# The seven products of the up projection in another order, on one core

## The chip, the cores and the metric

The kernel runs on one core of a Trainium2 chip. What is measured is the device time of one execution in microseconds (us). The kernel before takes 2845.7 us (median of three runs, 2845.06 to 2845.85).

## The reference

One layer of a hybrid decoder on 512 prompt tokens and 8 sample tokens, all in float32: attention and a gated branch side by side, an output projection, then a feed-forward part. Only the first step of the feed-forward part is touched:

```python
h = rmsnorm(x, lw['ffn_norm_w']) @ lw['w_up']        # 2048 -> 2 x 5632
...
hc = cw[0] * hp[:, 0:L] + cw[1] * hp[:, 1:L + 1] + cw[2] * hp[:, 2:L + 2] + lw['conv_b']
hg, hu = jnp.split(hc, 2, axis=-1)
x = x + (jax.nn.silu(hg) * hu) @ lw['w_down']
```

## The kernel before

All weights come from memory as blocks of 8 tiles of 128x128 (512 KB). For each block that TensorE multiplies with, ACT makes a rounded copy `hi` (`cast_block`, L246) and DVE the remainder `lo` (`rest_block`, L252); a product uses both. `hi` and `lo` have three buffers each, so ACT may begin the copy of block w+2 when TensorE leaves block w-1.

The up projection runs over 44 pairs of output tiles. Each pair (a **turn** below) is done with a scheme of seven products in place of eight (`winograd` for the weights, `wpair` for the matmuls, L353). A product is one block: 8 tiles, three matmuls each, 24 matmuls of 128x260. The turn reads four raw blocks: r11, r21, r22, r12. Tile `L` starts as r11, tile `S` as r21, both with two buffers; r12 and r22 come into plain tiles `st` (three buffers). Products P1 and P7 use `L`, P5, P6 and P3 use `S`, P2 uses r12 and P4 uses r22. In between the tiles are changed in place:

- first sum: `S` += r22, an accumulating DMA of POOL (L274), before P5
- second sum: `S` += `L`, an addition on DVE (L276, "vsum"), between P5 and P6
- `L` += r21, an accumulating DMA of POOL, between P1 and P7
- third sum: `S` += r12, an accumulating DMA of POOL, between P6 and P3

The order is written by hand. `acts[w]` lists what happens at the start of block w; with v the number of the turn's first block, the entries stand at v-8 to v+1. `block_start` (L258) issues them: loads on SP (L264), then what was left for this block, then the copy of block w+2 on ACT and its remainder on DVE, and behind these the sums of the block (L274, L276), POOL's small preparations `hb` (L1257, L1258) and SP's store `fd` of a finished turn (L1298). Every engine and both DMA queues take their instructions in this order. A load on SP waits until the last user of its buffer is through.

The products of a turn share four accumulators; after a product ACT or DVE takes the running value (`snap` L364, L368, L372, L376, L377). P1, P6 and P7 share bank a, so P6 cannot start before P1's value is copied out. Beside the products DVE and ACT work off the convolution of the turn before (L1263 to L1286). `w_out`, the stage ahead, builds the operands X of the seven products in the order of `PRODUCTS` (L405, L406, L414 to L425).

Of the kernel before, what the change touches and what calls it, by code (L numbers as in the profile page):

```python
# [17 lines left out]
S = 512  # L18
# [28 lines left out]
GV_TILES = tuple(range(20, 28))  # L47
MIX_TILES = (Q_TILES[0],) + sum(((Q_TILES[i + 1], GV_TILES[i]) for i in range(7)), ()) + GV_TILES[7:] + GU_TILES
FF_CHUNKS = (11, 11, 11, 11)
PRODUCTS = ("P5", "P1", "P2", "P6", "P4", "P7", "P3")  # L50
BANK = {"P5": "b", "P1": "a", "P2": "c", "P6": "a", "P4": "d", "P7": "a", "P3": "b"}
KQ = KD // 2

# [25 lines left out]
class Stream:  # L79
# [28 lines left out]
    def winograd(self, name, n1, n2, ks):  # L108
        assert not self.open and len(ks) == 2 * BLK
        v = len(self.keys)  # L110
        r11, r21, r22, r12 = (self.block([(name, k, n) for k in kk])
                              for kk, n in ((ks[0::2], n1), (ks[0::2], n2), (ks[1::2], n2), (ks[1::2], n1)))
        for p in PRODUCTS:
            self.vblock([(name, p, n1, i) for i in range(len(ks) // 2)],
                        {"P1": ("L", r11), "P7": ("L", r11), "P2": ("st", r12), "P4": ("st", r22)}.get(p, ("S", r21)))
        acts = self.acts
        acts[v - 8].append(("load", "S", r21, r21))
        acts[v - 7].append(("sum", "S", r21, r22))
        acts[v - 6].append(("load", "L", r11, r11))
        acts[v - 4].append(("load", "st", r12, r12))  # L120
        acts[v - 2] += [("load", "st", r22, r22), ("vsum", "S", r21, ("L", r11))]
        acts[v - 1].append(("sum", "L", r11, r21))
        acts[v + 1].append(("sum", "S", r21, r12))

    def done(self):
        assert not self.open
# [45 lines left out]
class Kernel:  # L172
# [180 lines left out]
    def wpair(self, name, n1, n2, X):  # L353
# [21 lines left out]
        def c12():  # L375
# [5 lines left out]
                 "P3": [("dve", c12)]}  # L381
        for p in PRODUCTS:
            z = BANK[p]
# [797 lines left out]
    def w_out(self):  # L1181
# [12 lines left out]
        X, build = self.woperands(xb)  # L1194
        X.update({p: [None] * KQ for p in PRODUCTS})
        todo = [(p, i) for p in PRODUCTS[:5] for i in range(KQ)] + [(p, i) for i in range(KQ) for p in PRODUCTS[5:]]
        early = [(p, i) for i in range((KD - OUT_GROUP) // 2) for p in ("P5", "P1")]
# [39 lines left out]
        self.finish_fine()  # L1237
        while todo[0][0] in PRODUCTS[:3]:
            build(*todo.pop(0))
# [304 lines left out]
```

## Time and profile before

| | before |
|---|---|
| median of three runs | 2845.7 us |
| the profiled execution's own time | 2843.6 us |
| its span | 2841.9 us |
| granted TensorE clock, mean | 0.994 |
| TensorE busy | 2771.4 us (98%) |
| DVE busy, ACT busy | 1564.8 us, 1090.1 us |
| up projection on TensorE | from 1157.15 to 2116.25 us |

Times within the profile are in us from the start of the span. In the rows of the timeline stand the start, the busy time, engine, line, operation, what is written and read, how many instructions were merged, and in brackets the idle time ahead and what ended it. In the chain of waits a row gives start, length and what the chain passed through.

### The profile page before, as it was taken

Reading aid. Unit: us, or ns where it says so; the run is one execution under the profiler, and the core shown is the slowest. Engines: PE = TensorE matmul, PEld = TensorE weight load, DVE = VectorE, ACT = ScalarE, POOL = GpSimd, SP = SyncE. Lnnn points to the kernel's source line nnn. Section 1 sums busy time; section 2 is a strip of 40 time slices with the busy share of each in tenths; the row PEclk is TensorE's granted clock in tenths of the full one; section 3 lists DMA queues with packets and bytes.
Section 4 is the critical chain, followed back from the end, with each engine's and each line's share of the span. In section 5 each row is a group of like instructions: output and inputs, shape, how many; then the busy total and the mean of one; then the engine's idle time right before and its main releaser. Section 6 shows DMA issues by size and latency. Waiting matters only on the chain.

```text
span 2841.9 us, 53344 instructions
## 1 busy us (share of the span) xinstructions
PE 2771.4 (98%) x22836; PEld 2753.5 (97%) x22836; DVE 1564.8 (55%) x2309; ACT 1090.1 (38%) x1775; POOL 237.1 (8%) x381
## 2 busy tenths in 40 slices
PE   9999999999999999799999999999999999999999
PEld 9999999999999999799999999999999999999999
DVE  5666555443333434777777777777773333333533
ACT  5465542222222333545444454444452222232321
POOL 0111000000000000021112112112210000000000
PEclk9999999999999999899999999999999999999999
DMA  5223233222232345477777777767765333323232
GB/s 179 90 88 115 83 97 92 87 88 88 94 94 93 112 139 169 120 188 189 175 180 193 185 179 190 188 168 188 185 184 194 120 115 120 112 91 96 86 112 94
DMA packets 118095, 381.01 MB, mean 134 GB/s; under 512 B 13457, under 2 KB 14609, under 8 KB 117857
## 3 DMA queue, kind: packets, MB, share of 16 engines
q1 hardware_dynamic: 97344, 303.49, 33.0%
q0 software_dynamic: 20512, 74.11, 13.4%
q8 instruction: 179, 2.93, 0.4%
q14 instruction: 60, 0.48, 0.1%
HBM read 352.42 MB, written 25.12 MB: 133 GB/s over the span
## 4 chain that ended last, share of the span: by engine, by line
PE 66%; DMA 15%; DVE 8%; POOL 4%; issue 4%; ACT 2%; DVEq 0%; SPq 0%; ACTq 0%; POOLq 0%
PE mm L330 21%; PE mm L334 20%; PE mm L332 20%; DMA S<-in_w 15%; DVE lo L252 4%; POOL hb L1258 3%; ACT hi L246 2%; DVE S L276 2%; POOL S L274 1%; PE wa L391 1%; DVE hb L1283 1%; PE wb L391 1%; PE po L927 1%; PE s L864 1%; PE pt L909 0%
## 5 line engine op out<-in xcount | busy, mean ns | idle before, releaser
L252 DVE TENSOR_TENSOR lo<-st,hi 128x1024 fp32r<-128x1024 f32 (+1 forms) x398 | 484.8, 1219 | 591.9 <-ACT hi L246 589.9
L246 ACT CAST hi<-st 128x1024 fp32r<-128x1024 f32 (+1 forms) x398 | 415.2, 1044 | 746.7 <-PE mm L332 438.2
L330 PE MATMUL mm<-xnh,hi 128*128 128x260 f32 x1920 | 393.8, 287 | 5.2 <-ACT hi L246 5.2
L391 PE MATMUL wa<-X,hi 128*128 128x260 f32 x2112 | 388.1, 285 | 7.2 <-ACT sn L364 7.1
L332 PE MATMUL mm<-xnl,hi 128*128 128x260 f32 x1920 | 386.3, 282 | 0.0
L334 PE MATMUL mm<-xnh,lo 128*128 128x260 f32 x1920 | 386.3, 283 | 0.0
L391 PEld LDWEIGHTS wa<-X,hi 128*128 128x128 f32 x2112 | 326.5, 190 | 7.9 <-ACT sn L364 7.5
L330 PEld LDWEIGHTS mm<-xnh,hi 128*128 128x128 f32 x1920 | 295.2, 189 | 5.3 <-ACT hi L246 5.2
L332 PEld LDWEIGHTS mm<-xnl,hi 128*128 128x128 f32 x1920 | 299.5, 190 | 0.0
L391 PE MATMUL wa<-X,lo 128*128 128x260 f32 x1056 | 298.6, 283 | 0.0
L334 PEld LDWEIGHTS mm<-xnh,lo 128*128 128x128 f32 x1920 | 293.5, 188 | 0.0
L330 PE MATMUL mm<-fh,hi 128*128 128x260 f32 x1408 | 284.2, 283 | 3.5 <-DVE x L1378 3.5
L334 PE MATMUL mm<-fh,lo 128*128 128x260 f32 x1408 | 284.3, 283 | 0.0
L391 PE MATMUL wb<-X,hi 128*128 128x260 f32 x1408 | 264.9, 289 | 19.6 <-DVE xr L1208 9.6
L332 PE MATMUL mm<-fl,hi 128*128 128x260 f32 x1408 | 283.6, 283 | 0.0
L391 PEld LDWEIGHTS wb<-X,hi 128*128 128x128 f32 x1408 | 220.1, 192 | 26.3 <-ACT hi L246 16.0
L252 DVE TENSOR_TENSOR lo<-S,hi 128x1024 fp32r<-128x1024 f32 x132 | 158.0, 1223 | 141.2 <-ACT hi L246 137.6
L391 PE MATMUL wb<-X,lo 128*128 128x260 f32 x704 | 204.5, 290 | 28.4 <-DVE lo L252 28.4
L330 PEld LDWEIGHTS mm<-fh,hi 128*128 128x128 f32 x1408 | 217.6, 189 | 3.7 <-DVE x L1378 3.7
L334 PEld LDWEIGHTS mm<-fh,lo 128*128 128x128 f32 x1408 | 218.3, 189 | 0.0
L332 PEld LDWEIGHTS mm<-fl,hi 128*128 128x128 f32 x1408 | 217.3, 189 | 0.0
L391 PEld LDWEIGHTS wa<-X,lo 128*128 128x128 f32 x1056 | 200.2, 190 | 0.2 <-DVE lo L252 0.2
(287 smaller groups left out, 4951.6 us busy)
## 6 DMA issues: line engine op xcount, KB each, us to landing
st<-in_w SPq DMA_DIRECT2D x395, 512.0 KB, 3.6
S<-in_w POOLq DMA_DIRECT2D x88, 512.0 KB, 10.3
S<-in_w SPq DMA_DIRECT2D x44, 512.0 KB, 3.6
L<-in_w SPq DMA_DIRECT2D x44, 512.0 KB, 3.9
L<-in_w POOLq DMA_DIRECT2D x44, 512.0 KB, 8.3
fd<-hb SPq DMA_DIRECT2D x44, 260.0 KB, 2.2
fr<-fd SPq DMA_DIRECT2D x44, 260.0 KB, 4.0
x<-in_x SPq DMA_DIRECT2D x16, 260.0 KB, 6.1
```

Of the source, the lines that this page charges most:

```text
L246: self.nc.scalar.copy(self.hi[v][:, c], self.st[WS.src[v]][:, c])
L252: self.nc.vector.tensor_sub(self.lo[v][:, c], self.st[WS.src[v]][:, c], self.hi[v][:, c].bitcast(F32))
L274: self.nc.gpsimd.dma_start(self.st[kind, r], self.a["w"][src], accum_op=ALU.add)
L276: self.nc.vector.tensor_add(self.st[kind, r], self.st[kind, r], self.st[src])
L330: mm(ps[:, h, 0:HW], lhsT=whi, rhs=xh[:, h, :], start=start, stop=False)
L332: mm(ps[:, h, 0:HW], lhsT=whi, rhs=xl[:, h, :], start=False, stop=False)
L334: mm(ps[:, h, 0:HW], lhsT=wlo, rhs=xh[:, h, :], start=False, stop=stop)
L391: nc.tensor.matmul(ps(z), lhsT=w, rhs=x, start=new and i == 0 and q == 0, stop=i == len(X[p]) - 1 and q == 2, skip_group_check=True)
L864: nc.tensor.matmul(out, lhsT=self.cols(q, c), rhs=keys(kk, c), start=n == 0, stop=n == 1)
L927: nc.tensor.matmul(po[:, kb * 128:kb * 128 + w], lhsT=vv[:, kb * 128:(kb + 1) * 128], rhs=pp[:, o:o + w], start=kb == 0 and n == 0, stop=k ...
L1258: nc.gpsimd.tensor_copy(sv(k)[:, :, 0:2], self.sc[:, n, :].rearrange("p (b r) -> p b r", b=NS))
L1283: nc.vector.tensor_mul(fv[:, :, 0:HP], tg[:, 0:S].rearrange("p (h w) -> p h w", h=2), tu[:, 0:S].rearrange("p (h w) -> p h w", h=2))
```

## The change

The seven products are multiplied in the order P1, P5, P6, P2, P4, P7, P3 in place of P5, P1, P2, P6, P4, P7, P3. The load of `S` and its first sum stand one block earlier in the list; the vsum stands one block later, at v-1, ahead of the sum of `L`, which stays at v-1; the third sum stands one block earlier, at v. `w_out` builds the operands in the new order.

```diff
-PRODUCTS = ("P5", "P1", "P2", "P6", "P4", "P7", "P3")
+PRODUCTS = ("P1", "P5", "P6", "P2", "P4", "P7", "P3")
...
-        acts[v - 8].append(("load", "S", r21, r21))
-        acts[v - 7].append(("sum", "S", r21, r22))
+        acts[v - 9].append(("load", "S", r21, r21))
+        acts[v - 8].append(("sum", "S", r21, r22))
         acts[v - 6].append(("load", "L", r11, r11))
         acts[v - 4].append(("load", "st", r12, r12))
-        acts[v - 2] += [("load", "st", r22, r22), ("vsum", "S", r21, ("L", r11))]
-        acts[v - 1].append(("sum", "L", r11, r21))
-        acts[v + 1].append(("sum", "S", r21, r12))
+        acts[v - 2].append(("load", "st", r22, r22))
+        acts[v - 1] += [("vsum", "S", r21, ("L", r11)), ("sum", "L", r11, r21)]
+        acts[v].append(("sum", "S", r21, r12))
```

On DVE, around the vsum of one turn. Before (lo317 is P5, lo318 P1, lo319 P2, lo320 P6; L1283 and L1286 are the last step of the turn before, after which `fd` is stored; L372, L376 and L377 take accumulators of the turn before):

```order
L252 TENSOR_TENSOR lo317_17622<-S261_17403,hi317_17621 128x1024
L276 TENSOR_TENSOR S261_17403<-S261_17403,L260_17479 128x1024
L1283 TENSOR_TENSOR hb_1083_17451<-c1_1077_17311,c2_1080_17411 128x2x256
L1286 TENSOR_TENSOR hb_1083_17451<-c1_1077_17311,c2_1080_17411 128x2x4
L372 SCALAR_TENSOR_TENSOR c2_1090_17659<-wa_1084_17478,sn_1085_17481 128x260
L252 TENSOR_TENSOR lo318_17655<-L260_17479,hi318_17654 128x1024
L376 TENSOR_TENSOR c1_1087_17559<-wb_1082_17442,un_1089_17587 128x260
L377 TENSOR_TENSOR c2_1090_17659<-wd_1088_17586,un_1089_17587 128x260
L252 TENSOR_TENSOR lo319_17692<-st263_17549,hi319_17691 128x1024
L1263 TENSOR_TENSOR hb_1091_17687<-c2_1090_17659,R2_888_12943 128x512
L1264 TENSOR_TENSOR hb_1091_17687<-c2_1090_17659,R2_888_12943 128x8
L252 TENSOR_TENSOR lo320_17732<-S261_17403,hi320_17731 128x1024
```

Now, in the same place of the same turn on DVE (lo317 is P1, lo318 P5, lo319 P6, lo320 P2):

```order
L252 TENSOR_TENSOR lo317_17624<-L260_17480,hi317_17623 128x1024
L1283 TENSOR_TENSOR hb_1083_17452<-c1_1079_17344,c2_1080_17410 128x2x256
L1286 TENSOR_TENSOR hb_1083_17452<-c1_1079_17344,c2_1080_17410 128x2x4
L372 SCALAR_TENSOR_TENSOR c2_1090_17658<-wa_1082_17443,sn_1085_17482 128x260
L252 TENSOR_TENSOR lo318_17654<-S261_17373,hi318_17653 128x1024
L276 TENSOR_TENSOR S261_17373<-S261_17373,L260_17480 128x1024
L376 TENSOR_TENSOR c1_1089_17592<-wb_1084_17479,un_1087_17551 128x260
L377 TENSOR_TENSOR c2_1090_17658<-wd_1088_17586,un_1087_17551 128x260
L252 TENSOR_TENSOR lo319_17693<-S261_17373,hi319_17692 128x1024
L1263 TENSOR_TENSOR hb_1091_17688<-c2_1090_17658,R2_888_12948 128x512
L1264 TENSOR_TENSOR hb_1091_17688<-c2_1090_17658,R2_888_12948 128x8
L252 TENSOR_TENSOR lo320_17733<-st263_17549,hi320_17732 128x1024
```

The vsum has moved behind L1283, L1286, L372 and P5's remainder; P6's remainder has moved ahead of L1263, L1264 and P2's remainder.

On POOL, the same turn (S261 and L260) with the first sum of the next turn (S265). Before:

```order
L274 DMA L260_17479<-in_w 128x1024
L1257 MEMSET hb_1091_17687 128x2
L1258 COPY hb_1091_17687<-sct_12949 128x8x2
L274 DMA S265_17651<-in_w 128x1024
L1257 MEMSET hb_1093_17699 128x2
L1258 COPY hb_1093_17699<-sct_12949 128x8x2
L274 DMA S261_17403<-in_w 128x1024
```

And now on POOL:

```order
L274 DMA L260_17480<-in_w 128x1024
L274 DMA S265_17621<-in_w 128x1024
L1257 MEMSET hb_1091_17688 128x2
L1258 COPY hb_1091_17688<-sct_12954 128x8x2
L274 DMA S261_17373<-in_w 128x1024
L1257 MEMSET hb_1093_17700 128x2
L1258 COPY hb_1093_17700<-sct_12954 128x8x2
```

One pair of preparations now stands behind the third sum (S261) and no longer ahead of it. On SP the order of loads and stores within the turns is what it was.

## The prediction

> **What bounds the kernel now.** I read the busy times first, then the waits of TensorE, then the chain of waits through the stage that the change touches.
>
> ```profile
> PE 2771.4 (98%) x22836; PEld 2753.5 (97%) x22836; DVE 1564.8 (55%) x2309; ACT 1090.1 (38%) x1775; POOL 237.1 (8%) x381
> ```
>
> ```profile
> PE wb L391 <- DVE lo L252: 28.4, 39, 0.8
> PE wb L391 <- DVE xr L1208: 9.6, 1, 9.6
> PE wb L391 <- ACT hi L246: 9.3, 20, 1.0
> PE wa L391 <- ACT sn L364: 7.1, 2, 6.9
> ```
>
> TensorE sets the time, and nearly all that it waits for lies in the up projection (L391): twice some us at the entry, and then 39 times, about once a turn, for weights of bank b. Bank b serves P5 and P3. The idle time understates the loss, since ends of matmuls are modelled, so I take the spacing of turns from the chain of waits:
>
> ```profile
> 1186.99 5.73 PE wb L391 x48
> 1207.09 5.73 PE wb L391 x48
> 1227.19 2.88 PE wb L391 x24
> ...
> 2113.35 2.90 PE wb L391 x22
> ```
>
> The first three rows begin with P3 of turns 0, 1 and 2: 1207.09 - 1186.99 = **20.10 us** a turn, with no wait, 2.87 us a product. The last row is P3 of turn 43 from its third matmul (22 are left), which in turn 2 stood two matmuls (0.24 us of the 2.88) behind the start, at 1227.43. So 41 turns took 885.92 us where 41 x 20.10 = 824.1 would do: **61.8 us lost**, 1.5 a turn.
>
> ```profile
> 1229.89:1400.00 170.11, 162.89 (x1321) 160.20 (x1320) 124.64 (x174) 83.48 (x142) 34.48 (x56) 0.99 0.73 184
> 1800.00:2000.00 200.00, 190.90 (x1550) 187.80 (x1549) 146.34 (x201) 97.91 (x167) 38.44 (x63) 0.99 0.73 184
> ```
>
> In these two stretches the granted clock was 0.99 (third number from the end); 1% of 370 us is 3.7. I leave 3 us of the loss to the clock and count **58.5 us** as waits. What sets the 1.5 us shows the chain between two copies of P3's weights:
>
> ```profile
> by line: DMA S<-in_w 45.6%; issue 11.7%; DVE lo L252 11.3%; POOL hb L1258 8.3%; DVE S L276 5.2%; ACT hi L246 4.8%; POOL S L274 3.5%; DVE hb L1283 2.6%; PE wb L391 1.2%; POOL hb L1257 0.8%; DMA fr<-fd 0.6%; DVE c L372 0.6%; DMA st<-in_w 0.5%
> ...
> 1634.38 1.06 ACT hi L246
> ...
> 1645.43 10.11 DMA S<-in_w
> 1655.62 1.06 ACT hi L246
> ```
>
> It is a loop: the third sum lands, ACT copies P3's weights, DVE works through its queue up to P6's remainder, POOL issues the next third sum, which lands 10.11 us later. One turn of the loop is 1655.62 - 1634.38 = 21.24 us, more than TensorE's 20.10. So the loop sets the pace, and its parts are what the change is to be judged by.
>
> **The change, part by part.** I put 0 at 1634.38 and lay the new order on the rows of this turn.
>
> ```profile
> 1636.28 0.65 ACT L1279 ACTIVATE c<-c 128x536 f32<-128x536 f32 x1
> 1637.09 1.05 ACT L246 CAST hi<-L 128x1024 fp32r<-128x1024 f32 x1
> 1642.82 1.05 ACT L246 CAST hi<-S 128x1024 fp32r<-128x1024 f32 x1
> ...
> 1635.47 2.36 DVE L252 TENSOR_TENSOR lo<-S,hi 128x1024 fp32r<-128x1024 f32 x2 [3.54 <-ACT hi L246]
> 1637.86 1.22 DVE L276 TENSOR_TENSOR S<-S,L 128x1024 f32<-128x1024 f32 x1
> 1639.01 0.69 DVE L1283 TENSOR_TENSOR hb<-c,c 128x512 f32<-128x512 f32 x1
> 1640.15 1.21 DVE L252 TENSOR_TENSOR lo<-L,hi 128x1024 fp32r<-128x1024 f32 x1
> 1641.28 0.42 DVE L376 TENSOR_TENSOR c<-wb,un 128x260 f32<-128x260 f32 x1
> 1641.96 1.21 DVE L252 TENSOR_TENSOR lo<-st,hi 128x1024 fp32r<-128x1024 f32 x1
> 1643.91 1.23 DVE L252 TENSOR_TENSOR lo<-S,hi 128x1024 fp32r<-128x1024 f32 x1
> ```
>
> ```profile
> 1639.97 0.33 SPq L1298 DMA_DIRECT2D fd<-hb  x1
> 1640.39 0.38 SPq L264 DMA_DIRECT2D L<-in_w  x1
> 1640.82 2.70 SPq L264 DMA_DIRECT2D st<-in_w  x2
> ...
> 1641.66 0.87 POOL L274 DMA_DIRECT2D L<-in_w  x1 [17.05 <-DVE lo L252]
> 1643.16 0.86 POOL L274 DMA_DIRECT2D S<-in_w  x1
> 1645.43 0.86 POOL L274 DMA_DIRECT2D S<-in_w  x1 [0.26 <-DVE lo L252]
> ```
>
> *DVE up to the sum of L.* Remainders of P3 and the first product end at +3.45, as now (P1's in place of P5's, which has the same size). L1283 follows at +3.48, the time at which the vsum starts today; it needs L1279, which ends at 1636.93 = +2.55. From L1283 to the start of the next remainder are 1640.15 - 1639.01 = 1.14 us, so P5's remainder runs from +4.62 to +5.83; its copy, in the place of today's copy at 1637.09, ends at +3.76. The vsum then starts at +5.76 (starts here follow 1.14 apart) and ends at +6.98. The sum of `L` comes 0.30 us after the DVE row that frees it (1641.66 against 1640.15 + 1.21): **+7.28**, to the hundredth what it is today (1641.66). The vsum's move costs nothing there: the pieces only change places.
>
> *The third sum.* P6's copy waits for the vsum: +7.04 to +8.09. L376 and L377 (0.68 us up to the next start) fit beside it. P6's remainder runs +8.13 to +9.36; today it starts at 1643.91 = +9.53 and ends at +10.76, because P2's remainder (1641.96) and two rows of the convolution stand ahead and its copy (1642.82) must wait until TensorE has left P5. POOL follows 0.29 us behind: **+9.65 against +11.05**, 1.40 us sooner. POOL is free by then: the sum of `L` at +7.28, the next turn's first sum 0.87 behind, and one pair of preparations, which today lets the following sum start 2.27 us after the one before it (1643.16 to 1645.43, DVE's wait included). With today's 10.11 us it lands at +19.8 and the loop closes in **19.9 us, below 20.10**.
>
> *The queue under it.* The 10.11 us are no property of the sum alone:
>
> ```profile
> 1640.50:1645.00 4.50, 4.50 (x40) 4.50 (x40) 4.44 (x7) 1.44 (x3) 3.34 (x6) 1.00 0.89 279
> 1645.00:1651.00 6.00, 6.00 (x53) 6.00 (x52) 3.85 (x7) 3.05 (x6) 1.03 (x2) 1.00 1.01 239
> 1651.00:1654.50 3.50, 3.50 (x32) 3.50 (x31) 2.69 (x3) 1.43 (x5) 0.00 (x0) 1.00 1.03 207
> 1654.50:1658.00 3.50, 2.74 (x24) 2.49 (x22) 1.30 (x2) 2.38 (x3) 0.00 (x0) 1.00 0.05 8
> ```
>
> The last two numbers of a row are the busy share of the DMA engines and GB/s. From SP's store at 1639.97 until the third sum is in, the 16 DMA engines are full (shares 0.89, 1.01, 1.03, and 0.05 behind it): three loads, the store and three sums share them. So a sum issued sooner lands sooner only if the full stretch also starts sooner. It does: the store needs L1283, which moves from 1639.01 (+4.63) to +3.48, and the two loads behind it on SP move with it, 1.15 us. If the stretch keeps its whole length, the loop takes 21.24 - 1.15 = **20.09**. The second of the two `st` loads waits for P2's remainder, which now comes behind P6's, some 2.5 us later; that takes bytes from before the sums and can only help them. The load of `S` keeps its place: it waits for P3's remainder (+2.3) either way, and SP's order is the same. "A block sooner" is thus worth nothing for the load, and the first sum, 0.6 us earlier, is not waited for.
>
> The Trainium skill speaks against the change here ("Trainium Kernel Development and Optimization", Key Constraints): DMAs of SP, ACT and POOL run on the same 16 DMA engines and interleave, so issuing from several engines saves only issue time. The trace agrees that they are shared (share 1.01 with loads and sums together). By that rule alone the third sum would land as long after the sum of `L` as today, and nothing would be won; that is the second rival below.
>
> *TensorE's side.* If P3 starts at +1.1 (copy done) and ends at +4.95 (its remainder comes at +2.3), P6, now third, is due two products later, at 4.95 + 2 x 2.87 = +10.7; its weights are ready at +9.36, 1.3 us to spare. P1's value in bank a is copied out right behind P6's copy (+8.09), in time for it. Next late would be P6, then nothing: P7's `L` lands with the first of the three sums. Once TensorE is the slower one, the sums are issued earlier against its position and the margin of P3 grows. So the steady turn should be 20.1 us: **-58.5 us**.
>
> *The entry.* This happens once.
>
> ```profile
> 1175.68 0.80 PE L391 MATMUL wa<-X,hi 128*128 128x260 f32 x2 [6.86 <-ACT sn L364]
> 1174.02 1.33 ACT L405 CAST X<-xb 128x260 fp32r<-128x260 f32 x4 [3.93 <-DVE xb L425]
> 1171.94 1.77 DVE L456 RECIPROCAL ry<-rv 128x260 f32<-128x260 f32 x1
> ```
>
> The wait of 9.6 us is for the last tile of the stage ahead and stays. In turn 0 P6 waits 6.86 us for P1's copy, which stands on ACT behind operands X that hang on a reciprocal of 1.77 us. Now P1's copy comes a block sooner, ahead of that; P6 comes a product (2.87) sooner as well, and P4's weights meet the reciprocal instead. Bounds: 6.9 us gained (wait gone) to 5 us lost (P6 meets the operands of P2, P4 and its own, at 0.4 us a step, one block earlier). I take the value near the reciprocal: **-2 us**.
>
> **The sum.** Profiled execution: 2843.6 - 58.5 - 2 = 2783. The median of the runs (2845.7) lies 2.1 above it, so the forecast for the runs is **2785 us**, 2774 to 2797 with the entry's bounds, a few us of clock and single stalls.
>
> **The rivals.**
> - *The loop shortens but stays above 20.10.* For it: 20.09 is no margin, and the full stretch varies (the clock aside, a turn lost 1.5 us on the mean, this one 1.14). Against it: the freed `st` load. At the middle between 20.1 and 21.24, half of the gain remains: 2845.7 - 29 - 2 = 2815.
> - *The change moves the issue and not the landing.* If the queue is served in order from the sum of `L` on, the third sum lands 1655.6 - 1641.66 = 13.9 us behind it. That issue stays at +7.28, so the loop stays 21.2: 2844, no change. Against it: SP's loads, which fill the first part of that stretch, do move.
> - *Slower: the vsum holds the sum of `L`.* It now stands directly ahead of it, behind P5's remainder, which can be copied only once TensorE has left P7. If that chain on DVE slips, the sum of `L` and the two behind it slip too. It decides from +7.28 plus what the stretch gains (1.15), +8.4; a slip of 1.15 + 1.22 (one more vsum's length) gives 41 x 1.22 = 50 us: 2896. Against it: the copy at +3.76 is 0.9 us ahead of DVE.
>
> **How the numbers follow.** Forecast 0.70, partial loop 0.15, landing unmoved 0.08, slower 0.07. The range takes the forecast whole with 2 us of the entry's lower end, and the partial case but its worst third: 2772 to 2828. A measurement of this kernel can tell about 0.2% (5.7 us) from no change: faster 0.85, same 0.08, slower 0.07.
>
> **What would show it.** Right: turns spaced 20.1 us, no waits of bank b for `lo` or `hi` in the steady state, ACT's copy of P3 no longer the last thing ahead of TensorE, the third sum issued 1.4 us sooner after P3's copy. Wrong: the sum of `L` issued later than +7.3 against P3's copy; a third sum that takes over 11 us; a new wait of bank a (P6) in every turn; P3 of turn 0 later than 1191, where it stood at 1186.99.

## The result, and the profile after

| | before | after |
|---|---|---|
| median of the runs | 2845.8 us (4 runs, 2845.1 to 2847.1) | 2798.5 us (4 runs, 2789.0 to 2799.9) |
| ratio of the times, 95% interval | | 0.9826 [0.9804, 0.9848] |
| profiled execution, its span | 2843.6 us, 2841.9 us | 2797.9 us, 2796.1 us |
| granted clock | 0.994 | 0.995 |

The kernel is 47 us faster, 13 less than the 60 that were forecast. It lies between the forecast (2785) and the first rival (2815: the loop shortens but stays above TensorE's pace).

From the page of the changed kernel its line of busy times, and then its waits of TensorE:

```profile
PE 2756.6 (99%) x22836; PEld 2747.3 (98%) x22836; DVE 1566.4 (56%) x2309; ACT 1091.2 (39%) x1775; POOL 218.4 (8%) x381
```

```profile
PE wb L391 <- DVE lo L252: 9.3, 16, 1.1
PE wa L391 <- DVE xr L1208: 9.0, 1, 9.0
...
PE wa L391 <- ACT sn L364: 3.6, 1, 3.6
...
PE wb L391 <- ACT hi L246: 1.7, 3, 0.8
```

Waits of bank b for `lo` have fallen from 39 times to 16, those for `lo` and `hi` together from 37.7 us to 11.0, but they have not gone. The starts of the turns tell it better than idle time. From the start of turn 1 to that of turn 43 the 42 turns took 59.9 us more than 42 x 20.10 before and take 20.7 us more now. Sixteen turns run at 20.13 or 20.14 us, without a wait; 26 take 20.2 to 23.5, and what they wait for is P3's weights. Turn 0 went from 32.5 to 29.5 us. These two make 42 of the 46 us between the profiled executions; the last turn gives 0.8, and most of the rest is that the up projection begins 2.3 us sooner (1154.88 against 1157.15); that start varies between 1154.9 and 1158.8 over all profiled kernels of this document, in both orders, and is not put down to the change.

One turn of the loop, in the timeline of the changed kernel, from P3's copy on ACT to the next (0 at 1587.05, as the prediction counted):

```profile
1587.05 1.05 ACT L246 CAST hi<-S 128x1024 fp32r<-128x1024 f32 x1 [4.38 <-DMA S<-in_w]
...
1589.76 1.05 ACT L246 CAST hi<-S 128x1024 fp32r<-128x1024 f32 x1
1594.15 1.05 ACT L246 CAST hi<-S 128x1024 fp32r<-128x1024 f32 x1 [3.33 <-DVE S L276]
...
1607.57 1.05 ACT L246 CAST hi<-S 128x1024 fp32r<-128x1024 f32 x1 [4.36 <-DMA S<-in_w]
```

```profile
1590.41 0.68 DVE L1283 TENSOR_TENSOR hb<-c,c 128x512 f32<-128x512 f32 x1
...
1591.56 1.22 DVE L252 TENSOR_TENSOR lo<-S,hi 128x1024 fp32r<-128x1024 f32 x1
1592.81 1.23 DVE L276 TENSOR_TENSOR S<-S,L 128x1024 f32<-128x1024 f32 x1
...
1595.23 1.23 DVE L252 TENSOR_TENSOR lo<-S,hi 128x1024 fp32r<-128x1024 f32 x1 [0.52 <-ACT hi L246]
```

```profile
1591.38 0.33 SPq L1298 DMA_DIRECT2D fd<-hb  x1
1591.80 0.38 SPq L264 DMA_DIRECT2D L<-in_w  x1
1592.23 6.39 SPq L264 DMA_DIRECT2D st<-in_w  x2
```

```profile
1594.57 0.86 POOL L274 DMA_DIRECT2D L<-in_w  x1 [17.42 <-issue]
1595.10 1.22 POOL L274 DMA_DIRECT2D S<-in_w  x1
...
1596.75 1.16 POOL L274 DMA_DIRECT2D S<-in_w  x1
```

The engines do what was worked out: L1283 at +3.36 (forecast +3.48), the vsum at +5.76 (+5.76), P6's remainder at +8.18 (+8.13), the third sum at +9.70 (+9.65). But P3's next copy comes at 1607.57 = +20.52 and not at +19.9: the third sum lands 10.7 us after its issue, where it was 10.1. The DMA engines are as full as before:

```profile
1592.00:1597.00 5.00, 5.00 (x44) 5.00 (x43) 4.45 (x7) 2.38 (x3) 2.43 (x5) 1.00 0.92 293
1597.00:1603.00 6.00, 6.00 (x52) 6.00 (x52) 5.31 (x9) 4.27 (x9) 1.32 (x4) 1.00 1.04 204
1603.00:1606.50 3.50, 3.50 (x31) 3.50 (x31) 2.36 (x4) 0.21 (x3) 0.00 (x0) 1.00 0.89 227
1606.50:1610.00 3.50, 3.39 (x29) 3.18 (x27) 1.35 (x2) 2.43 (x3) 0.00 (x0) 1.00 0.03 6
```

### The profile page after: what moved, and what is told of

It is laid out like the page before. It is cut to its first block, busy times and chain, and to the rows that moved or that the text cites. A ratio compares the mean times of both kernels' runs of the same rounds, so it can differ in the third digit from the quotient of the medians.

```text
span 2796.1 us, 53337 instructions
## 1 busy us (share of the span) xinstructions
PE 2756.6 (99%) x22836; PEld 2747.3 (98%) x22836; DVE 1566.4 (56%) x2309; ACT 1091.2 (39%) x1775; POOL 218.4 (8%) x381
## 3 DMA queue, kind: packets, MB, share of 16 engines
q0 software_dynamic: 20512, 74.11, 13.9%
## 4 chain that ended last, share of the span: by engine, by line
PE 75%; issue 16%; DMA 5%; POOL 2%; DVE 2%; ACT 1%; SPq 0%; POOLq 0%; ACTq 0%; DVEq 0%
PE mm L330 21%; PE mm L334 21%; PE mm L332 21%; DMA S<-in_w 4%; PE wa L391 4%; PE wb L391 3%; POOL S L274 1%; PE wc L391 1%; PE wd L391 1%; DVE lo L252 1%; POOL hb L1258 1%; PE po L927 1%; ACT hi L246 1%; PE s L864 1%; POOL L L274 1%
## 5 line engine op out<-in xcount | busy, mean ns | idle before, releaser
L391 PE MATMUL wa<-X,hi 128*128 128x260 f32 x2112 | 389.9, 285 | 12.7 <-DVE xr L1208 9.0
L246 ACT CAST hi<-S 128x1024 fp32r<-128x1024 f32 x132 | 138.5, 1049 | 304.3 <-DMA S<-in_w 153.0
```

Source lines behind the costliest of these rows:

```text
L246: self.nc.scalar.copy(self.hi[v][:, c], self.st[WS.src[v]][:, c])
L391: nc.tensor.matmul(ps(z), lhsT=w, rhs=x, start=new and i == 0 and q == 0, stop=i == len(X[p]) - 1 and q == 2, skip_group_check=True)
```

## The experiments

Each ran three rounds beside the kernel before, whose medians on those chips were 2843.6 to 2845.6 us. The theories in the expectations: **Q**, the full DMA engines decide when the third sum lands; **I**, it lands a fixed time after its own issue, which the new product order moved. The others are named where they stand.

**e1: the first sum behind the third.** Against the changed kernel:

```diff
-        acts[v - 8].append(("sum", "S", r21, r22))
+        acts[v - 7].append(("sum", "S", r21, r22))
```

> The changed kernel with the first sum back at v-7, where it now stands on POOL directly behind the third sum of the turn before it, no longer ahead of it. Theory Q (the DMA engines are full from the loads to the third sum, so what stands ahead of the third sum decides when it lands): 512 KB less ahead of it, about 2.5 us sooner, at some 12.5 to 13 us after the start of the turn in place of 13.5 to 17; no P3 waits, turns of 20.13 us, 2798 - 20 = 2778 us (2774 to 2786). Rival I (the landing follows the third sum's own issue by 10 to 11 us, and the new product order moved that issue): issue unchanged at +4.6, time unchanged, 2798 us.

Measured: **2778.7 us**, ratio to before 0.9768 [0.9754, 0.9783]. TensorE does not wait in the steady turns: it is busy throughout these windows, and the two sums of `S` now go out together, the third first:

```profile
1190.00:1390.00 200.00, 200.00 (x1672) 200.00 (x1671) 161.91 (x220) 109.63 (x181) 43.21 (x70) 1.00 0.78 196
...
1790.00:1990.00 200.00, 200.00 (x1671) 200.00 (x1670) 161.39 (x218) 107.37 (x179) 43.07 (x70) 1.00 0.79 198
```

```profile
1592.06 0.86 POOL L274 DMA_DIRECT2D L<-in_w  x1 [15.53 <-issue]
...
1594.25 1.76 POOL L274 DMA_DIRECT2D S<-in_w  x2 [0.26 <-DVE lo L252]
```

The time is Q's. The landing was sooner than expected, mostly 10 to 11 us after the start of the turn (median 10.0, latest 12.6) and not 12.5 to 13. So the "block sooner" of the first sum does harm: it puts 512 KB ahead of the sum that is waited for.

**e4: r22's load behind that of the next S**, so that it runs in the idle time behind the third sum. No sum is moved:

```diff
-        acts[v - 2].append(("load", "st", r22, r22))
-        acts[v - 1] += [("vsum", "S", r21, ("L", r11)), ("sum", "L", r11, r21)]
+        acts[v - 1] += [("load", "st", r22, r22), ("vsum", "S", r21, ("L", r11)), ("sum", "L", r11, r21)]
```

> The changed kernel with the load of r22 one place later on SP, behind the load of the next S, so that it runs while the DMA engines are idle and no longer beside the sums. No sum is moved. Theory Q: 1.5 us of work leaves the full stretch ahead of the third sum, which lands about 1 us sooner; most P3 waits go: 2778 to 2790 us. Rival I: the third sum's issue is unmoved, 2798 us.

Measured: **2781.4 us** [ratio 0.9759, 0.9792]. A plain load that nobody waits for, taken out of the stretch, is worth 17 us, and no sum goes out sooner for it (the third 6.4 us behind the store, 5.4 in the changed kernel): Q.

**e5: e1 and e4 together.**

> e1 and e4 together: first sum behind the third and r22's load behind that of the next S. In e1 TensorE already runs its turns at 20.13 us without a wait, so Theory Q expects nothing more: 2778 us (2775 to 2782). A rival that sees e1's and e4's gains as two separate ones would expect 2798 - 20 - 17 = 2761 us.

Measured: **2778.7 us** [ratio 0.9757, 0.9786], as e1 alone; the two cure the same wait.

**e2: the old order, the first sum a block sooner.** One part of the change alone, on the kernel before (load at v-9, first sum at v-8):

> The kernel before with one part of the change alone: load and first sum of S one block sooner. Theory Q and rival I agree: the third sum's issue (+11 us after the copy of P3) and the bytes ahead of it stay, so 2845 us (2840 to 2850). Rival F (the gain came from the first sum begun sooner): about 2800 us.

Measured: **2846.9 us**, ratio 1.0007 [0.9997, 1.0016]. This part of the change is worth nothing.

**e3: the old order, the first sum behind the third.**

```diff
-        acts[v - 7].append(("sum", "S", r21, r22))
+        acts[v - 6].append(("sum", "S", r21, r22))
```

> The kernel before, old product order, with the first sum one block later (v-6), so that it stands behind the third sum on POOL. Theory Q: the third sum lands about 2.5 us sooner, P3 no longer waits, but P5 follows directly and waits for the first sum that is now last; the loop closes over P5 at about 20.0 to 20.4 us: 2790 to 2805 us. Rival I (the product order is what counts, the issue of the third sum is unmoved): 2845 us, or slower by what P5 waits.

Measured: **2796.4 us** [ratio 0.9813, 0.9842], in the range of Q. One place in POOL's queue gives the old product order the same gain as the whole change. The waits that are left stand elsewhere than expected: about half of them at P1, the product behind P5, and hardly any at P5 itself; why is open.

**e9: the old order, the vsum one block later.**

```diff
-        acts[v - 2] += [("load", "st", r22, r22), ("vsum", "S", r21, ("L", r11))]
-        acts[v - 1].append(("sum", "L", r11, r21))
+        acts[v - 2].append(("load", "st", r22, r22))
+        acts[v - 1] += [("vsum", "S", r21, ("L", r11)), ("sum", "L", r11, r21)]
```

> The kernel before, old product order, with one thing of the change: the vsum one block later, behind the last step of the turn before (L1283) and P1's remainder, still ahead of the sum of L. The store and the two loads behind it on SP go out 1.15 us sooner after P3's copy; the sum of L stays at about +7.3 us, the third sum at about +11. Theory Q with the start of the full stretch as what counts: the loop shortens by about 1.1 us and sits at 20.1 to 20.6: 2800 to 2815 us. Rival L (the order of the sums from the sum of L on is what counts): 2845 us.

Measured: **2797.2 us** [ratio 0.9815, 0.9844], 3 us better than Q's range and level with the change (2798.5). Its timeline: P3's copy (first of the two in the row), SP and POOL, and the next copy of P3:

```profile
1594.90 2.00 ACT L246 CAST hi<-S 128x1024 fp32r<-128x1024 f32 x2 [2.52 <-DMA S<-in_w]
...
1599.22 0.33 SPq L1298 DMA_DIRECT2D fd<-hb  x1
...
1602.29 0.86 POOL L274 DMA_DIRECT2D L<-in_w  x1 [15.18 <-DVE S L276]
...
1603.56 0.86 POOL L274 DMA_DIRECT2D S<-in_w  x1
...
1606.32 0.86 POOL L274 DMA_DIRECT2D S<-in_w  x1 [1.66 <-DVE lo L252]
...
1615.48 2.00 ACT L246 CAST hi<-S 128x1024 fp32r<-128x1024 f32 x2 [3.03 <-DMA S<-in_w]
```

The third sum goes out 7.1 us after the store (1606.32 - 1599.22), 1.7 later than in the changed kernel (1596.75 - 1591.38 = 5.4), and P3's copy follows the store by 16.3 us against 16.2 there (1607.57 - 1591.38). Its later issue cost next to nothing. Counted from P3's copy, medians over the steady turns, the three sums stand where they stood before: 7.4, 8.7 and 11.1 us against 7.3, 8.8 and 11.1. The store and the two loads right behind it go out 1.26 us sooner (here 1599.22 - 1594.90 = 4.32 against 5.59), and the third sum lands at 20.5 in place of 21.5. So rival L falls as well: the landing does not keep its distance from the sum of `L`, and it is the earlier start of the stretch that gains.

**e10: the old order with e4's move of r22's load** (from v-2 to v, behind the next `S` on SP).

> The kernel before, old product order, with the load of r22 behind the load of the next S on SP (e4's edit on the old order): 512 KB of loads go out of the full stretch into the time in which the engines are idle. Theory Q: the third sum lands 1 to 1.5 us sooner, the loop sits at 20.1 to 20.3 and most of P3's waits go: 2787 to 2800 us. Rival P (the product order is needed for the gain): 2840 us or more.

Measured: **2808.9 us** [ratio 0.9856, 0.9886]. Rival P falls, but Q's number was 9 us too low: the landing moved 0.9 us against the store, not 1 to 1.5, which leaves a loop of 20.7.

**e12: the old order with e9 and e3 together.**

> The old product order with the vsum one block later (as in e9) and the first sum behind the third (as in e3). Theory Q: the third sum is out of the loop; what closes it now is the first sum, which lands about 16.0 us after the store, and P5's copy and remainder, which in the old order stand ahead of L1283 and the store: 16.0 + about 3.5 = 19.5 us, below TensorE's 20.1, so nearly all turns without a wait, and the entry of the old order (turn 0 some 3 us longer): 2781 to 2790 us. Rival O (the new product order is needed to get below 2797): 2795 us or more.

Measured: **2782.8 us** [ratio 0.9770, 0.9802]. No steady turn waits in the old product order either, and of the 4 us to e1 its longer turn 0 is 2.6 (32.1 against 29.5).

**e6 and e7: a slip of 1.2 us.** P5's remainder is computed twice over, ahead of the vsum and so of all three sums, in the changed kernel (e6) and in e1 (e7):

```diff
             elif what == "vsum":
+                self.rest_block(v + 2)
```

> The changed kernel with P5's remainder computed twice over on DVE, directly ahead of the vsum: 1.2 us more on DVE ahead of the vsum, the sum of L and the two sums behind it, nothing else (this is the slip that the prediction priced as its slower case, 1.22 us). Theory Q with a loop of 20.4 us against TensorE's 20.13: there is no margin left, so most of the 1.2 us shows in each turn: 0.8 to 1.2 us x 41, 2830 to 2848 us. Rival M (TensorE sets the pace and the waits left are single hiccups of DMA): the slip is hidden in most turns, 2798 to 2815 us.

> The same slip of 1.2 us in the kernel of e1 (first sum behind the third). There the third sum lands at about +10 to +11 after the start of the turn and may land as late as +15, so Theory Q has about 4 us of margin and the slip costs nothing: 2778 to 2784 us. If the slip costs 40 us here as well, DVE and not the queue is what limits, and Theory Q falls.

Measured: **2837.4 us** for e6, 39 us more than without the slip (0.95 us a turn), and **2782.4 us** for e7, 4 more, none of it in the steady turns (41 of 42 still run at 20.13 or 20.14 us). The changed kernel has hardly any margin; e1 has more than 1.2 us.

**e11: the slip behind the sum of `L`**, so that it holds the third sum alone:

```diff
             if what == "sum":
+                for _ in range(1 if kind == "S" and src == r + 2 else 0):
+                    self.rest_block(v + 2)
```

> The changed kernel with P6's remainder computed twice over on DVE: the third sum is issued 1.2 us later, while the sum of L and the first sum ahead of it stay. It is the slip of e6 behind the sum of L in place of ahead of it, and takes the place of e8, whose edit hardly moved the issue. Theory Q (the engines come to the third sum only about +10 to +11 after the start of the turn, whenever it was issued): 2796 to 2806 us. Rival I (landing = own issue + about 10.7 us): 1.2 us in each of 41 turns as in e6, 2838 to 2848 us.

Measured: **2812.2 us** [ratio 0.9871, 0.9904], between the two. One turn, from P3's copy to the next (lines of `kernel.py` behind the edit are numbered two higher here):

```profile
1595.88 1.05 ACT L246 CAST hi<-S 128x1024 fp32r<-128x1024 f32 x1 [3.60 <-PE wd L393]
...
1600.21 0.33 SPq L1300 DMA_DIRECT2D fd<-hb  x1
...
1603.40 0.86 POOL L276 DMA_DIRECT2D L<-in_w  x1 [14.92 <-issue]
...
1607.09 0.86 POOL L276 DMA_DIRECT2D S<-in_w  x1 [1.70 <-DVE lo L252]
...
1616.80 1.05 ACT L246 CAST hi<-S 128x1024 fp32r<-128x1024 f32 x1 [4.38 <-DMA S<-in_w]
```

The same slip costs 39 us ahead of the sum of `L` and 14 behind it. Q is right on which counts, but a third of the slip shows in the time, and why is open: P2's remainder and with it r22's load slip as well.

**e8: the third sum put back one block**, at v+1, in the changed kernel.

> The changed kernel with the third sum alone put back one block (v+1, behind P2's remainder and two rows of the convolution), in the new product order. Its issue moves some 2.2 us later (from about +4.6 to +6.8 after the start of the turn); the sums ahead of it and the loads stay. Theory Q (the full DMA engines decide when it lands): the engines come to the third sum only at about +10 to +11 after the start, so it lands where it does now and the time stays near 2798 us (2792 to 2808). Rival I (landing = own issue + 10 to 11 us): 2.2 us more in each of 41 turns, 2798 + 90 = 2888 us, at least 2850.

Measured: **2804.3 us** [ratio 0.9847, 0.9884]. It tells nothing between Q and I, since the edit did not do what was expected of it: POOL waits for P6's remainder alone and not for what stands ahead of the line in the list, so the third sum went out 0.3 us later (5.7 after the store against 5.4) and not 2.2. e11 took its place.

Over the steady turns (from the third on) of the kernels whose third sum is waited for, medians of the starts in SP's and POOL's rows and of the landing, all from the issue of the store; the last column is the median from the sum's own issue to its landing:

| | sum of `L` issued | third sum issued | third sum landed | its own time |
|---|---|---|---|---|
| before | 1.7 | 5.5 | 15.9 | 10.4 |
| e2 | 1.7 | 5.5 | 15.9 | 10.4 |
| after | 3.2 | 5.4 | 16.0 | 10.6 |
| e8 | 3.2 | 5.7 | 16.1 | 10.4 |
| e9 | 3.1 | 6.7 | 16.2 | 9.3 |
| e11 | 3.2 | 6.9 | 16.4 | 9.5 |
| e6 | 4.5 | 6.6 | 17.1 | 10.4 |
| e10 (512 KB less) | 1.7 | 5.5 | 15.0 | 9.5 |

The landing stands 15.9 to 16.4 us behind the store, whether the third sum goes out 5.4 or 6.9 us behind it. What moves it is 512 KB less in the stretch (e10), and a sum of `L` that comes later still (e6: 1.3 us later, landing 1.1 later). From the sum of `L` to the landing it is 14.2 us before, but 12.8 after and 12.7 in e6: in the changed kernel the sum of `L` has come to hold the landing too. Whether a store that goes out still sooner would bring more there was not run.

## Why the prediction was right, and where it was short

- **What bounds the kernel** was right: the loop over the third sum. Where it is cut (e1, e5, e12) the steady turns fall to 20.1 us. A small slip in its sum: 61.8 less 3 for the clock is 58.8, not 58.5; nothing hangs on it.
- **DVE up to the sum of `L`** was right to 0.1 us, but for POOL's part: the sum of `L` went out at +7.52 and not +7.28, since POOL needed 0.53 us behind the vsum where it needed 0.30 behind a remainder.
- **The third sum, 1.40 us sooner**: it went out at +9.70 as forecast, and that was worth little: e9 has the gain without it, and holding the third sum back by 1.5 us in e11 cost 0.3 us a turn, with r22's load held back as well. The 19.9 us drawn from it with a fixed 10.11 us was wrong. The Trainium skill ("Trainium Kernel Development and Optimization", Key Constraints) says that DMAs of SP, ACT and POOL share the same 16 DMA engines, so that issuing from several engines saves only issue time. The runs agree in so far as the third sum's later issue in e9 (6.7 us behind the store against 5.5 before) cost next to nothing. The rival that the prediction built beside it, a landing that keeps its 13.9 us behind the sum of `L`, fell all the same, because the loads ahead of the sums moved too: 14.2 us before, 12.8 after.
- **The queue under it** named the true gain: store and loads 1.15 us sooner. P3's copy to the store went from 5.59 us (1639.97 - 1634.38) to 4.33 (1591.38 - 1587.05). e9 has this alone, in the old order, and gets the whole gain.
- **The step that was mis-sized** is what that term was taken from: "If the stretch keeps its whole length, the loop takes 21.24 - 1.15 = 20.09". The stretch did keep its length (15.9 us from the store to the landing before, 16.0 after), and the loop did shorten by 1.2 us in the median, but the turn at 1634.38 was a short one: its sum landed 15.6 us behind the store (1645.43 + 10.11 - 1639.97), and its 21.24 us stand against a median of 21.6 from copy to copy. Now it is 4.3 us from P3's copy to the store and 16.1 from there to the next copy, a loop of 20.44, above TensorE's 20.10 to 20.13: some 14 us over 42 turns. From it followed the second error, "the margin of P3 grows": a loop as long as TensorE's turn has no margin, and its landings vary: 13.5 to 17.1 us after the start of the turn, where P3, due at 6 x 2.87 = 17.2 with 2.4 us of copy and remainder ahead of its third matmul, starts to wait from about 15. A late landing costs time and an early one gives none back, since no turn is shorter than 20.13. So 20.7 us of the 59.9 stayed. The text had said that 20.09 is no margin and had given that case 0.15; it deserved the most.
- **The `st` load that comes 2.5 us later** shows no gain: it goes out 6.9 us behind the store, 4.4 in e9, and the landings are the same (16.0 and 16.2). It still lies inside the stretch (its issue ends at 1592.23 + 6.39 = 1598.6, while the sums run). Only taking it out of the stretch gained (e4, e10).
- **"A block sooner" is worth nothing for the load and the first sum**: right for the old order (e2). In the new one, where the third sum stands a block sooner too, it costs some 20 us, because it keeps the first sum ahead of the third (e1).
- **The entry**: -2 us forecast, -3.0 measured on turn 0, and P6's wait for P1's value fell from 6.9 to 3.6 us. All kernels with the new order have a turn 0 of 29.5 us (30.8 in e11), all with the old one 32.1 to 32.7. This is all that the new product order itself was seen to give.
- **The slower rival**, a slip ahead of the sum of `L`: the mechanism is real: a slip of 1.2 us costs 0.95 us a turn (e6). Its threshold was wrong: it was to begin at +8.4, and nearly all of a slip from +7.5 to +8.8 shows. So the price beyond the threshold was not tested by itself.

## What to carry to other kernels

When transfers of several queues fill the DMA engines, do not add a transfer's usual time to its issue: find where the full stretch begins and what must pass ahead of the one that is waited for. Then either begin the stretch sooner (e9), move a sum that is needed later behind the one that is waited for (e3), or take a load out of the stretch (e10); each of the three was worth 37 to 48 us on the kernel before, alone, and e1's one line on top of the change brings 2798.5 down to 2778.7.
A loop that is worked out to equal the engine's own pace is not cured: take its length from the median of many turns, and count on half of the turns to come late.

## What was not expected of the hardware

The accumulating DMAs use the engines far less well than plain loads. In the kernel before, two windows with sums alone (first and last row) and one with loads alone, all at or near a full share:

```profile
1192.50:1194.50 2.00, 2.00 (x19) 2.00 (x19) 0.66 (x3) 1.32 (x2) 0.69 (x3) 1.00 0.95 158
1211.00:1213.00 2.00, 2.00 (x19) 2.00 (x18) 1.87 (x3) 0.14 (x1) 2.00 (x6) 1.00 1.04 358
1198.00:1202.00 4.00, 4.00 (x35) 4.00 (x35) 3.93 (x7) 2.35 (x5) 0.00 (x0) 1.00 1.06 211
```

Loads move 358 GB/s, sums 158 and 211. Over 800 us of steady turns (1300 to 2100, kernel before) the two queues stand like this, POOL's sums in q0 and SP's loads and stores in q1, with packets, MB and the share of the 16 engines' time:

```profile
q0 software_dynamic: 15990, 58.23, 38.4%
q1 hardware_dynamic: 26740, 86.89, 33.8%
```

From these two rows 512 KB take about 2.8 us of all engines as a sum (0.384 x 800 us for 58.23 MB) and 1.6 as a load, so three sums weigh as much as five loads.
